# The scan's state and output products in natural order of the heads

## The chip, the cores and the metric

The kernel runs on one core of one Trainium2 chip. The metric is the device time of one run in microseconds; before the change it is 3602.42 us, the median of three runs that lie between 3598.81 and 3608.07 us. Times of instructions come from one profiled execution of the same program, counted from its first instruction.

## The reference

The reference is a small network in float32 over 512 tokens of 1024 features and a context of 256 tokens: two layers of a first block (attention with latent keys, then a gated spatial layer, each with a large MLP) and four modulated layers of a second one (convolution, recurrent layer, attention, convolution). The change lies in the recurrent layer. There each of 16 heads keeps a state S of 64 x 64, and for each token in turn, once forward over the tokens and once backward:

```
sa  = S @ (-kk_t)
S   = S * d_t  +  sa (x) (kk_t * a_t)  +  v_t (x) k_t
out = S @ r_t
```

Here d_t is a decay for each key feature, and (x) an outer product. Context tokens come first, then the others, so 768 tokens in each direction.

## The kernel before, in words

The layers run one after another. The recurrent layer writes its inputs for the scan (arrays krd, bkd, vd) to memory, and the function `wkv` reads them back and scans. It doesn't go token by token: 768 tokens are 12 chunks of 64, and within a chunk the recurrence is solved by products of matrices and the inverse of a triangular 64 x 64 matrix for each head and direction.

The work is cut into eight segments: four groups of three steps (a step is one chunk) by two halves of the heads (g, eight heads each). Both directions of a step are done side by side, each with its own chunk. Segments alternate between the halves of the heads, so that the next segment can be prepared while the present one is scanned.

`prepare` makes a segment ready. For each of its three steps it loads BK (line 1161), KR (line 1164; two loads for a direction, `for e in range(2)`, one for the place of the even heads and one for that of the odd heads in each pair) and UV (line 1155), all from the queue of SyncE. TensorE then forms G (line 1177, in two PSUM buffers) and transposes BK (line 1187); VectorE masks G into GA (line 1184). VectorE inverts the 32 x 32 diagonal blocks of all heads in a long chain of small operations (lines 1205 and 1207) between transposes of 32 x 32 (lines 1198, 1217, 1222). KR has one buffer for each half of the heads, so a load for the segment after next goes where the present segment's KR has been read for the last time.

`merge` puts the inverses of the 64 x 64 matrices together from the 32 x 32 ones with small products (lines 1233 and 1240); it needs the transposes of line 1222.

`chain` does the three steps of a segment. In each step, for both directions:

- X (lines 1264 and 1266): two products a head, accumulated in the lower 64 partitions of a PSUM tile; ScalarE copies it (line 1268).
- U (line 1271): one product a head into the upper 64 partitions, which ScalarE copies into UV (line 1272).
- S, the step of the state (line 1280): one product a head, which ScalarE scales in four pieces of two heads (line 1283) and GpSimd adds to what is left of the old state (lines 1255 and 1285).
- O, the output (lines 1288 and 1290): two products a head (one in the first step, where there is no state), copied by ScalarE (line 1292) and written out by SyncE's queue (line 1296). The last step has no S.

S and O share one tile of PSUM for each direction, `so`. Head h writes the partitions `hr(h)`: the lower 64 for an even head, the upper 64 for an odd one. In a product of TensorE the partitions of the output are the columns of its array, so even heads use columns 0 to 63 and odd heads columns 64 to 127; all 128 rows are used by both. Every product here is in float32 and shows as two records in the trace, each with a load of weights.

The order of S and O over the heads is the tuple EO (line 1121): (0, 2, 4, 6, 1, 3, 5, 7). It is used at lines 1279 and 1287.

After each step `beside` calls the generators of the next two segments' preparation, so that their work lies beside the scan. The order of instructions on each engine is set by a planner of the language when the program is built: it follows dependencies and its own costs, and may put a block of preparation into the middle of a step. In the program as built, the first G block of a preparation stands on TensorE between the first direction's X and the second direction's X of the next step, or after the first half of a merge.

Of the kernel before, what the change touches and what calls it, by code (L numbers as in the profile page):

```python
# [51 lines left out]
class Stream:  # L52
    """Pools and helpers for a chain of layers over N tokens, features on the partitions."""
# [8 lines left out]
    def pools(self, nm, wst=0, whl=0, hp=0, tp=0, mm=0, W=None, hw=None):  # L62
        """Opens the pools that are asked for by their buffers."""
# [23 lines left out]
    def wblk(self, src, cols=1024, st=None):  # L87
        """A block of weights in float32, split exactly into two float32r parts."""
        nc = self.nc
        st = self.load(src, cols) if st is None else st  # L90
        hi = self.whl.tile([P, 1024], F32R, name="wh")[:, :cols]
        lo = self.whl.tile([P, 1024], F32R, name="wl")[:, :cols]
        nc.scalar.activation(out=hi, in_=st, func=AF.Copy)  # L93
        (nc.gpsimd if self.pool_lo else nc.vector).tensor_tensor(out=lo, in0=st, in1=hi.bitcast(F32), op=ALU.subtract)  # L94
        if self.tick:
            self.tick()
        return hi, lo
# [5 lines left out]
    def split(self, pr, src, scale=None, bias=None):  # L103
        """hi + lo = src * scale, or src + bias"""
# [20 lines left out]
    def lin(self, outs, w, acts, wo=0, ws=P, start=True, stop=True):  # L125
        """outs: [(PSUM part, columns of the tokens)]"""
# [14 lines left out]
    def group(self, ws, acts):  # L141
        """Several outputs at once, as the operands become ready."""
# [6 lines left out]
    def rsqrt(self, v, pool=None):  # L149
        """v ** -0.5 on a small tile [128, n]"""  # L150
# [14 lines left out]
    def colsum(self, tiles, N):  # L165
        """Sums over the features for each token: PSUM [128 tokens, N / 128]."""
# [8 lines left out]
    def rows(self, y, N, tag="rs", dst=None):  # L175
        """Columns y [128 tokens, N / 128] -> a row over all partitions [128, N]; in PSUM without a tag."""
# [33 lines left out]
class Kern:  # L210
# [17 lines left out]
    def open_x(self, n):  # L228
        """The two streams and the running sums of their squares."""
# [12 lines left out]
    def track(self, k, vi=0, acc=None, gain=1.0):  # L242
        """x[:, k] is final: its squares go into the sum for the next norm."""
# [14 lines left out]
    def both_rstd(self, s):  # L258
        """The norms of x and of the context in one chain."""
# [18 lines left out]
    def set_filler(self, gen, per=1):  # L278
        """Another chain of work, emitted in step with the blocks of weights of the main one."""
# [14 lines left out]
    # ------------------------------------------------------------- modulation  # L294
# [7 lines left out]
    def modulation(self, s, l, pool, ps):  # L302
        """shift, scale and gate of layer l, for both vectors, with the features on the partitions"""
# [28 lines left out]
    def mod_h(self, s, x, l, vi, rs=None, gs=None):  # L332
        """The modulated norm of x, split."""
# [17 lines left out]
    # -------------------------------------------------------------- conv layer  # L351
    def conv(self, s, x, l, j, vi):
# [3 lines left out]
        with self.tc.tile_pool(name=f"cv{N}", bufs=1, side=s.side, reuse_waits="tile") as cp, \  # L356
# [5 lines left out]
            for k in range(KT):  # L362
# [10 lines left out]
                # twice a * sigmoid(b)  # L373
# [18 lines left out]
            # layer norm over the features  # L392
# [25 lines left out]
            # the norm that the next layer starts from takes the place of the sums  # L418
# [3 lines left out]
    def conv_x(self, l, j):  # L422
        """The layer on x. The convolution runs in PSUM: some taps as diagonal matrices on TensorE, most on VectorE; the last ones are for ScalarE and GpSimd."""
        nc, A, s, x, N, H = self.nc, self.A, self.m, self.x, T, 15
        NPE, NPO, NG = 4, 7, 4
        with self.tc.tile_pool(name="cv", bufs=1, reuse_waits="tile") as cp, self.tc.tile_pool(name="cw", bufs=5, reuse_waits="tile") as cw, \
# [7 lines left out]
            def glu(k):  # L434
# [7 lines left out]
                # twice a * sigmoid(b)  # L442
# [60 lines left out]
            # layer norm over the features  # L503
# [23 lines left out]
    # ---------------------------------------------------------------- block 1  # L527
    def scaled(self, gname, gi):
        """x * gain, split"""
# [15 lines left out]
    def mla(self):  # L545
        nc, tc, A, s = self.nc, self.tc, self.A, self.m
        scale = 192.0 ** -0.5
        with tc.tile_pool(name="mla", bufs=1, reuse_waits="tile") as mp, tc.tile_pool(name="mla2", bufs=2, reuse_waits="tile") as m2, \
# [10 lines left out]
            # the first products wait in PSUM for the norm  # L559
# [6 lines left out]
            # rope tables: cos and signed sin of fl(position * inv_freq)  # L566
# [160 lines left out]
    def sgu(self):  # L727
        nc, tc, A, s = self.nc, self.tc, self.A, self.m
        with tc.tile_pool(name="sgu", bufs=1, reuse_waits="tile") as sp, tc.tile_pool(name="sgu2", bufs=2, reuse_waits="tile") as s2, \
                tc.tile_pool(name="sgu8", bufs=9, reuse_waits="tile") as s8, s.pools("m", hp=8, tp=2, mm=2), tc.tile_pool(name="pa", bufs=1, space=PSUM, reuse_waits="tile") as pa:  # L730
            # spatial weights, masked, and the sums of their rows
# [76 lines left out]
    def final_norm(self, s):  # L808
        """The norm at the end of the first block, and in one step with it the norm of the layer that follows."""
# [6 lines left out]
        # r1 = (m1 + eps) ** -0.5 and r1 * (r1 ** 2 * m2 + eps) ** -0.5 = (m2 + eps * (m1 + eps)) ** -0.5  # L816
# [16 lines left out]
    # -------------------------------------------------------------- rwkv layer  # L833
    # tokens of both sequences side by side: 256 of the context, then 512 of x; two halves of 384 in two banks
# [8 lines left out]
    def headcols(self, pq, y, yw, dst):  # L843
        """y [128 tokens, 6 blocks, n heads] -> [64, 768 tokens]: rows from 0 and from 32 hold the two exact parts"""
# [10 lines left out]
    def headrows(self, pq, yr, hrow):  # L855
        """[64, 768 tokens] of headcols -> a row for each of two heads, as hrow selects them: PSUM [128, 2, 384]"""
# [5 lines left out]
    def rwkv_project(self, kd, vd, gd, bd, krd, bkd, pc, xd, xcd):  # L862
# [6 lines left out]
        with tc.tile_pool(name="pj", bufs=1, reuse_waits="tile") as pj, s.pools("r", wst=3, whl=2, mm=2), \  # L869
# [12 lines left out]
            with tc.tile_pool(name="p1", bufs=1, reuse_waits="tile") as p1:  # L882
                h = p1.tile([P, KT, TJ], F32, name="h")
                xx = p1.tile([P, KT, TJ], F32, name="xx")
                def lerp(i, half, tp):
                    """Half of the tiles: the second half takes buffers that the layer before has to leave."""
                    return [lerp1(i, k, tp) for k in range(4 * half, 4 * half + 4)]
# [25 lines left out]
                with s.pools("rn", tp=2, W=T):  # L913
                    # mu / 2 and 1 - mu for the first product, which then need not wait for xx
# [37 lines left out]
                with tc.tile_pool(name="p2", bufs=2, reuse_waits="tile") as p2:  # L952
# [18 lines left out]
                    # the values with the tokens on the partitions  # L971
# [35 lines left out]
                    # the rest of them finds its place when h and xx are gone  # L1007
                    rawp = right("raw")
                    raws = [lerp1(5, k, rawp, raw=True) for k in range(4, 8)]
            with tc.tile_pool(name="hp2", bufs=1, reuse_waits="tile") as hp2:  # L1010
# [5 lines left out]
                with tc.tile_pool(name="p3", bufs=1, reuse_waits="tile") as p3, tc.tile_pool(name="p4", bufs=2, reuse_waits="tile") as p4:  # L1016
                    def small(m):
                        """w2 and a2, split, and the rows that select the heads"""
# [6 lines left out]
                    # a running sum over each chunk starts from a zero in front of it, or behind it  # L1025
# [3 lines left out]
                    # a0 / 2, w0 / 2, k_a / 2 and 1 - k_a / 2, and the constant of the decay  # L1029
# [28 lines left out]
                    def chunks(m, k, r, wa):  # L1058
                        pr = self.headrows(pq, kyr, wa[0][:64, 256:])
                        # half of the normalised k  # L1060
# [41 lines left out]
                        # bonus: sum over the head of r * (both k) * r_k, times v, left for the scan that has the time  # L1102
# [13 lines left out]
    def wkv(self, vd, bd, krd, bkd, pc, od, osp):  # L1116
        nc, tc = self.nc, self.tc
        NS, NU = 3, 24
        # where the inverses pause
        CUT = (10, 20)  # L1120
        EO = (0, 2, 4, 6, 1, 3, 5, 7)
        chunk = lambda d, st: st if d == 0 else (3 - st if st < 4 else 15 - st)
        states, kept, first, last = {}, {}, [], {}
        with ExitStack() as c:
            pool = lambda n, b, **k: c.enter_context(tc.tile_pool(name=n, bufs=b, **k, reuse_waits="tile"))
            # the order of the pools puts what the first segment starts with where the layer before leaves first
# [7 lines left out]
            def prepare(g, b):  # L1134
                # 24 units forward, 8 that stay empty, 24 backward
                if b == 0:
# [3 lines left out]
                    # the two heads of a tile on the diagonal  # L1140
# [10 lines left out]
                def values(i):  # L1151
                    # V below an empty U
# [5 lines left out]
                for i in range(NS):  # L1158
# [6 lines left out]
                    # those of the first segment are behind all else that it loads  # L1165
# [5 lines left out]
                    for d in range(2):  # L1171
                        mask = self.c("mrev" if d else "mfwd")
                        for mm in range(2):
# [8 lines left out]
                            # nothing slows the inverses that the first step waits for  # L1182
# [8 lines left out]
                # inverses of the 32 x 32 diagonal blocks, one for a partition  # L1191
# [20 lines left out]
                for d in range(2):  # L1212
# [6 lines left out]
                    # the other orientation of the block that the merge starts from  # L1219
# [24 lines left out]
            def chain(beside, g, b, GA, KR, BT, UV, TP):  # L1244
                hr = lambda h: slice(64 * (h % 2), 64 * (h % 2) + 64)
                for i in range(NS):
                    st = NS * b + i
                    S0 = [states.get((g, d)) for d in range(2)]
                    # what is left of the state after this step
# [8 lines left out]
                    for d in range(2):  # L1258
                        # X in the lower half of the partitions, U in the upper
                        X = pch.tile([P, 8, 64], F32, name=f"xu{d}")  # L1260
                        xu.append(X)
                        for h in range(8):
                            # the rows of U are still zero
# [9 lines left out]
                    for d in range(2):  # L1273
                        cc = chunk(d, st)
                        u0 = d * 32 + 8 * i
                        # the step of the state, and the output
# [31 lines left out]
            # the bonus in place, beside the first inverses  # L1308
# [20 lines left out]
            for n, sg in enumerate(segs):  # L1329
                # the last step of the next segment and the start of its inverses  # L1330
# [16 lines left out]
    def rwkv_readout(self, gd, bd, od, last, xd, xcd):  # L1347
# [3 lines left out]
        # the order of the pools puts what the first half of the heads needs where the last segment of the scan has nothing,  # L1351
        # so that it runs beside the scan
        with ExitStack() as c:
# [23 lines left out]
            # the sums of squares of each head, for both halves of the heads  # L1377
            pk = s.mmt()[:, :96].rearrange("p (g b h) -> p g b h", g=2, h=8)

            def centre(g, m, pq):  # L1380
# [6 lines left out]
                # the centred o takes its place  # L1387
# [12 lines left out]
            def readout(g, i):  # L1400
                m = 4 * g + i
                # the backward o is no longer needed
# [499 lines left out]
```

## Time and profile before

| | |
|---|---|
| median of 3 runs | 3602.42 us |
| profiled execution, first to last instruction | 3582.6 us |
| TensorE busy in the profiled execution | 3409.4 us (95%) |
| VectorE busy | 2307.9 us (64%) |
| ScalarE busy | 1448.9 us (40%) |
| the scan's steps, about | 2135 to 2565 us of the span |

The profile gives no other time for the profiled execution than its span; the runs' times include what lies before the first and after the last instruction. A busy time is the union of an engine's instructions. Ends of TensorE's products are modelled, and they overlap, so a busy TensorE need not be one that works at its full rate: the distance between starts tells the rate. The clock is the share of TensorE's full clock that was granted. In a timeline, instructions of one form that follow each other are one row with their count, and a row ends with the engine's idle time before it and with what ended it.

### The profile page before, as it was taken

The numbers are of one execution on the slowest core, as the hardware profiler recorded it, in microseconds if no ns is written. First come the engines' busy times: TensorE is split into PE (matmuls) and PEld (weight loads), VectorE is DVE, ScalarE is ACT, GpSimd is POOL, SyncE is SP. The second block draws the span as 40 slices with busy tenths as digits, with TensorE's granted clock in tenths as the row PEclk, the third lists the DMA queues.
The fourth block names the chain that finished last, engine by engine and source line by source line (L and its number), as shares of the span: only waits on it lengthen the run. The fifth ranks groups of instructions, "written<-read, shape, count | busy, mean of one in ns | idle before, by whom it ended". The sixth has DMA issues, their size and how long they took to land. (4 is left out here: it accounts for less than half of the span.)

```text
span 3582.6 us, 52130 instructions
## 1 busy us (share of the span) xinstructions
PE 3409.4 (95%) x20784; PEld 2778.1 (78%) x20784; DVE 2307.9 (64%) x3811; ACT 1448.9 (40%) x2336; POOL 603.8 (17%) x674
## 2 busy tenths in 40 slices
PE   7999999999999999998999979999889999999897
PEld 4678888767766787676988858888788788888676
DVE  4568875426443345887478788888452476666786
ACT  3443334323232233555356524333423254444553
POOL 1000000000000000763002231121110200000682
PEclk9999999999999999998999879999899999999999
DMA  6123333343444322221227772221421522211221
GB/s 246 44 89 107 111 117 113 136 142 136 152 143 157 120 98 94 71 77 65 95 101 227 240 208 82 84 87 49 175 92 42 182 71 80 71 62 46 91 73 57
DMA packets 201380, 396.94 MB, mean 111 GB/s; under 512 B 16624, under 2 KB 109552, under 8 KB 200112
## 3 DMA queue, kind: packets, MB, share of 16 engines
q1 hardware_dynamic: 161328, 287.56, 24.0%
q0 software_dynamic: 24880, 93.08, 7.8%
q10 hardware_dynamic: 14928, 12.98, 1.2%
q8 instruction: 163, 2.67, 0.3%
q14 instruction: 81, 0.66, 0.1%
HBM read 328.79 MB, written 58.46 MB: 108 GB/s over the span
## 5 line engine op out<-in xcount | busy, mean ns | idle before, releaser
L93 ACT ACTIVATE wh<-wst 128x1024 fp32r<-128x1024 f32 (+1 forms) x413 | 423.0, 1026 | 1100.5 <-PE pmm L122 728.8
L121 PE MATMUL pmm<-hh,wh 128*128 128x512 f32 (+1 forms) x1752 | 670.5, 384 | 4.2 <-ACT hh L108 3.6
L123 PE MATMUL pmm<-hh,wl 128*128 128x512 f32 (+1 forms) x1752 | 662.3, 379 | 4.3 <-POOL wl L94 4.3
L122 PE MATMUL pmm<-hl,wh 128*128 128x512 f32 (+1 forms) x1752 | 661.5, 378 | 2.7 <-DVE hl L109 1.9
L94 DVE TENSOR_TENSOR wl<-wst,wh 128x1024 fp32r<-128x1024 f32 (+1 forms) x347 | 406.8, 1173 | 348.8 <-ACT wh L93 348.3
L121 PEld LDWEIGHTS pmm<-hh,wh 128*128 128x128 f32 x1752 | 332.0, 190 | 90.5 <-ACT wh L93 13.4
L123 PEld LDWEIGHTS pmm<-hh,wl 128*128 128x128 f32 x1752 | 331.1, 189 | 73.1 <-POOL wl L94 6.0
L122 PEld LDWEIGHTS pmm<-hl,wh 128*128 128x128 f32 x1752 | 331.3, 189 | 67.5 <-issue 5.3
L465 DVE SCALAR_TENSOR_TENSOR acc<-yp,vec,acc 128x512 f32<-128x512 f32 x320 | 224.5, 751 | 20.6 <-PE acc L461 14.1
L94 POOL TENSOR_TENSOR wl<-wst,wh 128x1024 fp32r<-128x1024 f32 x66 | 161.5, 2460 | 425.7 <-ACT wh L93 405.3
L539 DVE TENSOR_TENSOR x<-pmm,x 128x512 f32<-128x512 f32 x88 | 60.7, 690 | 247.7 <-PE pmm L123 247.7
L121 PE MATMUL pmm<-uh,wh 128*128 128x512 f32 x512 | 200.5, 392 | 0.0
L123 PE MATMUL pmm<-uh,wl 128*128 128x512 f32 x512 | 199.7, 390 | 0.0
L122 PE MATMUL pmm<-ul,wh 128*128 128x512 f32 x512 | 199.3, 389 | 0.0
L84 POOL DMA_DIRECT2D wst<-mod_w x96 | 50.8, 530 | 562.7 <-PE pmod L312 512.4
L312 PE MATMUL pmod<-wst,cs 128*32 128x512 f32 x384 | 110.5, 657 | 19.1 <-DMA wst<-mod_w 18.9
L474 POOL TENSOR_TENSOR part<-part,tap 128x512 f32<-128x512 f32 x96 | 124.0, 1292 | 13.8 <-ACT part L472 7.5
L708 DVE SCALAR_TENSOR_TENSOR ft<-pmm,rs 128x512 f32<-128x512 f32 x64 | 44.0, 688 | 118.4 <-PE pmm L123 117.0
L381 DVE SCALAR_TENSOR_TENSOR Y<-yp,vec,Y 128x256 f32<-128x256 f32 x240 | 115.7, 482 | 6.2
L121 PEld LDWEIGHTS pmm<-uh,wh 128*128 128x128 f32 x512 | 96.2, 188 | 26.4 <-ACT wh L93 7.5
L123 PEld LDWEIGHTS pmm<-uh,wl 128*128 128x128 f32 x512 | 96.1, 188 | 20.2
L1177 PE MATMUL G<-KR,BK 128*128 128x256 f32 x384 | 102.0, 410 | 10.1 <-DMA KR<-krd 6.6
(673 smaller groups left out, 7503.5 us busy)
## 6 DMA issues: line engine op xcount, KB each, us to landing
wst<-mod_w POOLq DMA_DIRECT2D x96, 512.0 KB, 4.0
wst<-w_up SPq DMA_DIRECT2D x64, 512.0 KB, 3.2
wst<-w_down SPq DMA_DIRECT2D x64, 512.0 KB, 3.2
wst<-conv_in SPq DMA_DIRECT2D x48, 512.0 KB, 3.2
wst<-conv_in POOLq DMA_DIRECT2D x24, 512.0 KB, 3.6
BK<-bkd SPq DMA_DIRECT2D x48, 256.0 KB, 2.9
KR<-krd SPq DMA_DIRECT2D x96, 128.0 KB, 3.3
krd<-kr SPq DMA_DIRECT2D x14, 768.0 KB, 4.3
```

Of the source, the lines that this page charges most:

```text
L84: self.dma.dma_start(out=st, in_=src)
L93: nc.scalar.activation(out=hi, in_=st, func=AF.Copy)
L94: (nc.gpsimd if self.pool_lo else nc.vector).tensor_tensor(out=lo, in0=st, in1=hi.bitcast(F32), op=ALU.subtract)
L121: nc.tensor.matmul(out, w[0], a[0], start=start, stop=False)
L122: nc.tensor.matmul(out, w[0], a[1], start=False, stop=False)
L123: nc.tensor.matmul(out, w[1], a[0], start=False, stop=stop)
L312: nc.tensor.matmul(pm[n // 4][32 * q:32 * q + 32, :], self.cs[:, k, :], w[:, h * 512:(h + 1) * 512], start=k == 0, stop=k == KT - 1, skip_ ...
L381: nc.vector.scalar_tensor_tensor(out=acc, in0=yp[:, i:i + N], scalar=wc, in1=acc, op0=ALU.mult, op1=ALU.add)
L465: nc.vector.scalar_tensor_tensor(out=accs[k], in0=yps[k][:, i:i + N], scalar=weight(k, i), in1=accs[k], op0=ALU.mult, op1=ALU.add)
L474: nc.gpsimd.tensor_tensor(out=part, in0=part, in1=t, op=ALU.add)
L539: self.nc.vector.tensor_tensor(out=self.x[:, m], in0=pt, in1=self.x[:, m], op=ALU.add)
L1177: nc.tensor.matmul(G[:, 2 * q:2 * q + 2].rearrange("p e x -> p (e x)"), BK[:, d, i, m].rearrange("p a t -> p (a t)"), KR[:, d, i, m].rearr ...
```

## The change

Line 1121 gives EO another value, so that S and O take the heads in the order 0 to 7. Even and odd heads then follow each other, and with them the two halves of the columns. Everything else in the change removes comments and doc strings, with line numbers kept.

```diff
@@ wkv
         # where the inverses pause
         CUT = (10, 20)
-        EO = (0, 2, 4, 6, 1, 3, 5, 7)
+        EO = range(8)
         chunk = lambda d, st: st if d == 0 else (3 - st if st < 4 else 15 - st)
```

## Rows read from the trace of the kernel before

**Rows 1.** The first line of the page: span and instructions.
```profile
span 3582.6 us, 52130 instructions
```
**Rows 2.** Stretches of the scan: length, busy PE, PEld, DVE, ACT, POOL; granted clock, DMA share, GB/s.
```profile
2135.00:2565.00 430.00, 411.71 (x6261) 371.90 (x6259) 338.39 (x574) 165.31 (x422) 77.51 (x109) 0.95 0.25 81
2186.00:2468.00 282.00, 271.13 (x4132) 243.14 (x4132) 247.17 (x417) 107.13 (x280) 53.90 (x73) 0.98 0.26 80
```
**Rows 3.** Waits from 2135 to 2565: us in total, times, longest.
```profile
DVE GA L1184 <- PE G L1177: 30.2, 23, 2.9
...
PE so L1288 <- ACT S L1283: 8.1, 19, 0.5
```
**Rows 4.** Timeline of TensorE's products: S of one step and X after it.
```profile
2315.66 1.37 PE L1280 MATMUL so<-UV,BT 128*64 128x64 f32 x29
2316.81 0.27 PE L1264 MATMUL xu<-UV,GA 128*64 128x64 f32 x1
2316.86 0.22 PE L1280 MATMUL so<-UV,BT 128*64 128x64 f32 x1
2316.92 0.22 PE L1264 MATMUL xu<-UV,GA 128*64 128x64 f32 x1
2316.92 0.22 PE L1280 MATMUL so<-UV,BT 128*64 128x64 f32 x1
```
**Rows 5.** Timeline of TensorE's products: O of the same step and X after it.
```profile
2317.64 0.33 PE L1288 MATMUL so<-GA,UV 128*64 128x64 f32 x2 [0.39 <-ACT S L1283]
...
2318.27 0.28 PE L1290 MATMUL so<-KR,S 128*64 128x64 f32 x2
2318.39 0.34 PE L1288 MATMUL so<-GA,UV 128*64 128x64 f32 x4
2318.51 0.33 PE L1290 MATMUL so<-KR,S 128*64 128x64 f32 x4
...
2319.14 0.34 PE L1288 MATMUL so<-GA,UV 128*64 128x64 f32 x4
...
2320.66 0.27 PE L1266 MATMUL xu<-S,KR 128*64 128x64 f32 x1
```
**Rows 6.** Timeline of ScalarE: the scalings of the same step's S.
```profile
2316.66 1.74 ACT L1283 ACTIVATE S<-so,pc 128x64 f32<-128x64 f32 x8 [0.78 <-PE so L1280]
```
**Rows 7.** Timeline of SyncE's queue: the loads of KR after this step.
```profile
2318.82 1.35 SPq L1164 DMA_DIRECT2D KR<-krd  x2
...
2321.96 1.26 SPq L1164 DMA_DIRECT2D KR<-krd  x2
```
**Rows 8.** DMA issues from 2150 to 2500: count, KB each, median us to landing.
```profile
KR<-krd SPq DMA_DIRECT2D x64, 128.0 KB, 2.9
```
**Rows 9.** Timeline of TensorE's products: first G block after three steps.
```profile
2171.76 1.53 PE L1177 MATMUL G<-KR,BK 128*128 128x256 f32 x6 [1.37 <-DMA KR<-krd]
...
2322.90 1.99 PE L1177 MATMUL G<-KR,BK 128*128 128x256 f32 x8
...
2357.43 1.75 PE L1177 MATMUL G<-KR,BK 128*128 128x256 f32 x7 [0.81 <-DMA KR<-krd]
```
**Rows 10.** Timeline of TensorE's products: two merges, and the G in one.
```profile
2296.43 1.70 PE L1233 MATMUL tr<-TP,GA 32*32 32x32 f32 x48
2297.94 1.45 PE L1240 MATMUL tr<-GA,TP 32*32 32x32 f32 x40
2299.32 1.99 PE L1177 MATMUL G<-KR,BK 128*128 128x256 f32 x8
...
2515.39 0.78 PE L1233 MATMUL tr<-TP,GA 32*32 32x32 f32 x19 [4.24 <-DVE TP L1222]
```
**Rows 11.** Timeline of VectorE: transpose of the first direction ahead of a merge.
```profile
2290.59 1.99 DVE L1222 STREAM_TRANSPOSE TP<-LW 32x1024 f32<-32x1024 f32 x1
```
**Rows 12.** Stretches, with the columns of Rows 2: around a wait, and a drop.
```profile
2170.00:2180.00 10.00, 8.63 (x84) 7.17 (x82) 6.73 (x17) 1.77 (x3) 0.00 (x0) 1.00 0.36 114
2307.90:2311.30 3.40, 3.40 (x35) 3.40 (x34) 3.35 (x3) 0.59 (x1) 0.00 (x0) 0.50 0.00 0
```

## The prediction

> **What bounds the kernel now.** I read the page's first part for the whole (a span of 3582.6 us [rows 1]), then the stretches of the scan [rows 2], then who waits for whom there [rows 3], and last, instruction by instruction, one step of the scan on TensorE, ScalarE and the loading queue, and the ends of segments [rows 4 to 11]. The reader is to see that TensorE is the engine that paces the scan (411.7 of 430 us busy in it) and that VectorE is not far behind (247.2 of 282 us in the five segments from 2186 to 2468). So time taken off TensorE counts, but little can be taken off before something else is late.
>
> A step of the scan (12 steps, two halves of the heads, so 24 in all) runs on TensorE as X, U, S (line 1280), O (lines 1288, 1290). A product is two records. Inside one half of the columns records start every 0.058 us: an x2 row of O is followed by the next after 0.116 [rows 5]. When the other half's first products come within reach, the halves run at once: the x4 rows hold twice the records in the same 0.116, and at the end of S records of X (lower half) and of S (upper half) alternate, each half still at 0.058 [rows 4]. But this holds for the last four records of a half only: even heads of O start at 2317.64, odd ones at 2318.39, the next direction's even ones at 2319.14, and X after both directions at 2320.66, so 16 records cost 0.75 us, not 16 x 0.058 = 0.93. In S four blocks of 8 records take 2315.66 to 2316.81, 0.29 each.
>
> **The change part by part.** No instruction and no transfer is added or removed; the products of S and of O only change places. With heads in natural order a product of the other half is always next or next but one, within the reach of four records seen above, so I take both halves to run at 0.058 throughout.
>
> *S.* The first direction's last record now starts 0.74 us after the first (0.29 + 0.05 for a first load + 7 x 0.058); then 0.05 + 7 x 0.058 = 0.46. ScalarE's four scalings wait for all eight heads: they start at 2316.66 after idling for S, though heads 0 and 1, which the first of them reads, were through by 2316.3 (odd heads start at 2315.66 + 0.29, two records and 0.22 to the end of a record) [rows 4, 6]. O in turn waits for the scalings (19 waits on TensorE [rows 3]) and starts 0.98 us after ScalarE began. So O begins 0.28 us earlier. TensorE's own end of S moves by more (0.35), which only lengthens the idle 0.39 before O. The second direction's scalings (1.74 us for eight) end 0.2 before its O is reached.
>
> *O.* From 2317.64 to X at 2320.66 are 3.02 us; then 32 records in each half, 32 x 0.058 + 0.05 = 1.91. Saving 1.11.
>
> *What is late next.* O is the last reader of KR, and its end releases the load of KR for the segment after next. That load feeds G (line 1177), which stands in TensorE's queue behind the first direction's X, and X's second direction, U and S are queued behind G. The two loads of a direction (even heads' place, odd heads' place) are issued at 2318.82 and, as the pair takes 1.35 with 0.6 each, at about 2319.57 [rows 7]. The even heads end no earlier than before: their 16 records take 0.05 + 15 x 0.058 from O's start either way. So the first load is issued at the same distance from O's start, and the second follows at the queue's own pace (the other direction's pair takes 1.26, so 0.66 apart instead of 0.75): 0.07 to 0.09 earlier. With 2.9 us to landing [rows 8] it lands near 4.75 us after O's start, and I let G start 0.1 after that (a guess at how long a wait takes to end), at 4.85. TensorE reaches G 5.26 us after O's start now (2322.90, no wait [rows 9]) and would at 4.15. So a step that doesn't wait today keeps 0.4 of the 1.11, and a step that waits already keeps 0.07. Ten steps have such a G; four of these start late by 0.35 to 1.4 (one, of 1.37, stands in [rows 9]); so 6 x 0.4 + 4 x 0.07 = 2.7 us. Bounds for one step: 0.07 and 1.11; I stay by the measured landing.
>
> Six steps end a segment: between O and G there stand 2.9 us of the merge (2296.43 to 2299.32 [rows 10]), and the load has landed. There O's 1.11 is kept, if VectorE's transposes for the merge are there. Where those for the first direction end at 2292.6, 3.8 before the merge, they are [rows 11]. I count three steps in full; the other three at 0.25 each (one already waits 0.81 for KR [rows 9]; two more I take like it, because VectorE, idle for 34.8 of 282 us [rows 2], will not follow everywhere): 3 x 1.11 + 0.75 = 4.1 us.
>
> The segment from 2468 to 2515 ends with TensorE waiting 4.24 us for VectorE [rows 10]: what its three steps save (2 x 1.39 + 1.11 = 3.9) only lengthens this wait. Zero.
>
> The last segment has no G and no inverses on VectorE: 3 x 1.11 = 3.3. The first steps of the first two segments have no state yet, so O has half the records: 0.2 each, 0.4.
>
> S's 0.28 falls in 22 steps, less the two in the segment that waits for VectorE: 20 x 0.28 = 5.6.
>
> Sum: 5.6 + 0.4 + 2.7 + 4.1 + 3.3 = 16.1 us. The profiled span of 3582.6 becomes 3566.5. The runs' median 3602.4 lies 19.8 above that span, outside of what changes: 3586.
>
> *Not shown in the trace:* the two halves alternating for longer than four records. Below I bound it from no overlap at all (a loss) to 0.029 per record over both halves; 32-column products on one tile already come every 0.031 (48 records in 1.51 us up to the next group [rows 10]), so TensorE can take records nearly that fast. I take full overlap, since rows 4 show both halves at full pace.
>
> The Trainium skill speaks against this ("TensorE: Matmul & The Clock Gate", Part 3, The mechanism and what overlaps): a weight load overlaps a product in flight only if the row group differs, and here both halves use all 128 rows. The trace disagrees as far as it goes: S and X at 2316.8 to 2317.0 load and multiply side by side in the same rows [rows 4]. By that rule the sum would be the loss of rival C.
>
> **Rivals.**
> A, *KR's load is not in the way*: G is moved by the planner, or loads land earlier with a queue that is less crowded, and the ten steps keep 1.11 as well, the six merge steps too: 16 x 1.11 + 3.3 + 5.6 + 0.4 = 27.1 us, 3575. For it: VectorE is idle for 34.8 us in the five segments [rows 2], and over the scan it waits 30.2 for G [rows 3], so it can start earlier. Against: G already waits for KR in some steps.
> B, *O gains nothing before the last segment*: the loads or VectorE take all of it; 5.6 + 3.3 = 8.9, 3593.5. For it: VectorE's 88% in the five segments (247.2 / 282); a mask that comes late holds the second G.
> C, *the halves take turns*: products of the other half don't run under one in flight unless they were already waiting. Then O is 64 x 0.058 + 0.05 = 3.76 (0.74 more) and S's first direction ends after 0.92 instead of 0.74. 19 full steps and 2 half ones outside the waiting segment: 19 x 0.74 + 2 x 0.3 + 20 x 0.18 = 18 us slower, 3621. It decides once a record costs more than about 0.047 over both halves, today's mean in O (3.02 / 64). Against: rows 4 and 5.
> D, *the clock*: TensorE waits 0.6 us more at each of ten G's and its granted clock drops in each. A drop as at 2307.9 lasts 3.4 us at a granted 0.50 (1.2 GHz) with TensorE busy throughout [rows 12], half of which is lost: ten times 1.7, the gain is gone, 3603. For it: the clock already stands at 0.95 over the scan, with such drops in it [rows 2]. Against: the wait of 1.37 for KR at 2171.76 brought none, the stretch around it stands at 1.00 [rows 12].
>
> **How the numbers follow.** Forecast 0.50; A 0.15; B 0.17; C 0.10; D 0.08. A measurement of this kernel can tell about 0.3% (10.8 us) from no change. Faster by over that: most of the forecast case (0.43), A, a part of B: 0.60. Within: the rest of these and D: 0.27. Slower: C, and some weight for a planner that orders the rest less well: 0.13. The range 3570 to 3606 holds the forecast, A, B and D and leaves out C and a gain beyond A's. The likeliest case alone is 3581 to 3592.
>
> **What would show it.** S in 0.98 us and O in 1.91 us from first record to the next X, with x4 or single alternating rows throughout; O's wait for ScalarE starting 0.28 us earlier; KR's pair issued 1.2 us after O's start as now; G waiting for KR in nearly all ten steps, some 0.6 us each; the wait for the transposes at 2515 grown by 3 to 4 us. O longer than 3.02 us means C; no waits at G means A. The prediction is wrong if the planner changes the order of TensorE's queue elsewhere, which no row of before can show.

## The result, and the profile after

The change makes the kernel faster: a median of 3582.2 us over 11 runs (3570.81 to 3590.26) beside 3607.02 over 11 runs of the kernel before on the same chip (3588.28 to 3620.07). The ratio of the two on record is 0.9948, with a 95% interval of 0.9930 to 0.9965: 18.8 us less, between 12.6 and 25.2. The two medians alone lie 24.8 apart, at the far end of that interval. A second set of 12 runs (e5 below) gave 0.9943 [0.9924, 0.9962]. The forecast was 3586.

The page of the changed kernel begins with the span and with each engine's busy time, share and instructions. The count of instructions is that of [rows 1].

```profile
span 3575.3 us, 52130 instructions
...
PE 3388.1 (95%) x20784; PEld 2755.5 (77%) x20784; DVE 2307.4 (65%) x3811; ACT 1446.7 (40%) x2336; POOL 603.2 (17%) x674
```

PE is busy for 21.3 us less than before and its weight loads (PEld) for 22.6 less; VectorE, ScalarE and GpSimd are busy for what they were, within 2.2. The spans differ by only 7.3 us, less than the medians do: in every case with a listed profiled run the profile's span lies 1.7 to 1.8 below that run's time, so the execution behind the profile of before took some 3584.4, under each of the 92 runs of that kernel that stand beside the results (3587.24 to 3627.24). A second profile of it (e10) has a span of 3612.9.

The same stretches as in [rows 2], and the one after them; columns as there.

```profile
2135.00:2565.00 430.00, 399.76 (x6460) 354.68 (x6458) 348.05 (x587) 172.34 (x435) 80.39 (x113) 0.94 0.29 93
...
2186.00:2468.00 282.00, 263.19 (x4253) 232.46 (x4249) 250.73 (x420) 107.77 (x286) 54.02 (x74) 0.95 0.27 83
2468.00:2515.00 47.00, 39.84 (x760) 37.78 (x759) 43.94 (x75) 17.34 (x43) 7.82 (x12) 0.86 0.31 103
```

In the same 282 us PE is busy for 8 us less while 121 more records start, and VectorE for 3.6 more: more of the scan fits in, and VectorE is busy for 89% of the stretch instead of 88%. Now one step on TensorE, the one after the merge at 2297 [rows 4, 5]:

```profile
2316.12 1.15 PE L1280 MATMUL so<-UV,BT 128*64 128x64 f32 x32
2317.10 0.40 PE L1264 MATMUL xu<-UV,GA 128*64 128x64 f32 x4
2317.83 0.34 PE L1288 MATMUL so<-GA,UV 128*64 128x64 f32 x4 [0.33 <-ACT S L1283]
2318.00 0.29 PE L1290 MATMUL so<-KR,S 128*64 128x64 f32 x4
2318.12 0.33 PE L1288 MATMUL so<-GA,UV 128*64 128x64 f32 x4
...
2319.63 0.34 PE L1290 MATMUL so<-KR,S 128*64 128x64 f32 x4
2319.75 0.28 PE L1266 MATMUL xu<-S,KR 128*64 128x64 f32 x2
2319.87 0.28 PE L1264 MATMUL xu<-UV,GA 128*64 128x64 f32 x2
```

All of O is now x4 rows at 0.116 us, 0.029 for a record. From O's start to the next X are 1.92 us (3.02 before), from S's start to X 0.98, from S's start to O 1.71 (1.98). The next direction's X, which uses one half only, is back at x2 rows, 0.058 for a record. On ScalarE the scalings start 0.73 after S does, not 1.00 [rows 6]; on SyncE's queue the loads of KR start 1.18 after O does, as before [rows 7]:

```profile
2316.85 1.74 ACT L1283 ACTIVATE S<-so,pc 128x64 f32<-128x64 f32 x8 [0.51 <-PE so L1280]
```

```profile
2319.01 1.30 SPq L1164 DMA_DIRECT2D KR<-krd  x2
...
2321.52 1.27 SPq L1164 DMA_DIRECT2D KR<-krd  x2
```

The first G blocks of four steps, where [rows 9] had one without a wait (a block has 8 records; x1 and x2 are what short windows held of it). The row of 2322.72 names a VectorE instruction as the releaser, but the trace has the second load of KR land at 2322.62, 0.10 before:

```profile
2173.88 0.67 PE L1177 MATMUL G<-KR,BK 128*128 128x256 f32 x2 [1.14 <-DMA KR<-krd]
...
2270.50 0.45 PE L1177 MATMUL G<-KR,BK 128*128 128x256 f32 x1 [1.14 <-DMA KR<-krd]
...
2285.90 0.45 PE L1177 MATMUL G<-KR,BK 128*128 128x256 f32 x1 [0.63 <-DMA KR<-krd]
...
2322.72 1.97 PE L1177 MATMUL G<-KR,BK 128*128 128x256 f32 x8 [0.59 <-DVE LW L1207]
```

Waits from 2135 to 2565 (total, times, longest), to be read against [rows 3], and the wait at the merge that was 4.24 long in [rows 10]:

```profile
DVE GA L1184 <- PE G L1177: 23.1, 23, 6.6
...
PE tr L1233 <- DVE TP L1222: 8.7, 3, 6.9
PE so L1288 <- ACT S L1283: 7.9, 17, 0.6
...
PE G L1177 <- DMA KR<-krd: 5.3, 6, 1.1
```

```profile
2508.83 2.60 PE L1233 MATMUL tr<-TP,GA 32*32 32x32 f32 x45 [6.87 <-DVE TP L1222]
```

VectorE waits less for G (23.1 for 30.2), TensorE more for VectorE and for KR. (The row for KR holds five of the ten first G's; the other five stand under VectorE, like that of 2322.72, though each starts 0.10 to 0.14 after its load has landed. All ten sum to 8.9 us, 2.7 before.) The order of instructions on ScalarE, GpSimd and SyncE is that of before; on TensorE and VectorE the planner moved some. In the ten steps with a G after X, 38 records of X start between O and the first G block, 36 before, so one product of X more stands ahead of it; some merges are split elsewhere. (X has 64 records for both directions, so in either kernel this G stands inside the second direction's X, and not ahead of it as the description of the kernel has it.)

### The profile page after: what moved, and what is told of

It reads as the page before. It is cut to its first block, busy times and chain, and to the rows that moved or that the text cites. A ratio compares the mean times of both kernels' runs of the same rounds, so it can differ in the third digit from the quotient of the medians.

```text
span 3575.3 us, 52130 instructions
## 1 busy us (share of the span) xinstructions
PE 3388.1 (95%) x20784; PEld 2755.5 (77%) x20784; DVE 2307.4 (65%) x3811; ACT 1446.7 (40%) x2336; POOL 603.2 (17%) x674
## 5 line engine op out<-in xcount | busy, mean ns | idle before, releaser
L465 DVE SCALAR_TENSOR_TENSOR acc<-yp,vec,acc 128x512 f32<-128x512 f32 x320 | 224.5, 752 | 20.5 <-PE acc L461 14.1
```

The lines of the kernel that those rows point to most:

```text
L465: nc.vector.scalar_tensor_tensor(out=accs[k], in0=yps[k][:, i:i + N], scalar=weight(k, i), in1=accs[k], op0=ALU.mult, op1=ALU.add)
```

## Experiments

Each ratio is to runs of the kernel before on the same chip. "Full-clock time" is a run's time multiplied by its mean granted clock, so that a us at half clock counts as half a us; waits at full clock count in full. For one kernel it scatters far less than the time (standard deviation over the 12 runs of e5: 4.2 us against 9.0), so what differs from run to run is mostly the clock. It is 3463.0 (33 runs), 3462.9 (31) and 3464.3 (17) for the kernel before on three chips, and 3440.0 for the change.

**e1, S alone in natural order.**

```diff
-                        for h in EO:    # S, line 1279
+                        for h in range(8):
```

> Natural order in S alone, O still even heads first. My theory (TensorE's two halves overlap; O starts when ScalarE has scaled S): S takes 0.93 us from first to last start instead of 1.32, O starts 1.71 us after S instead of 1.98, nothing else moves, about 20 steps keep 0.28 us: 5.6 us less than before (0.16%), so too small to be told by time alone. Rival (what helps is the planner's other order of TensorE's queue, not the halves): the queue's order here is that of before, so no step gets shorter.

Median 3597.22 (12 runs), ratio 0.9983 [0.9968, 0.9997]: 6 us less (1 to 12), and 4.9 by full-clock time. In its profile S takes 0.93 us from first to last start in 17 of 22 steps (1.32 before), O stays at 3.19. The order of instructions is that of before on every other engine, and G stands where it stood in X, so this is the alternation and nothing else.

**e2, O alone.**

```diff
-                        for h in EO:    # O, line 1287
+                        for h in range(8):
```

> Natural order in O alone, S still even heads first. My theory: O takes 1.85 us to the next X instead of 3.02, but in the ten steps with a G block after X that block waits for the load of KR (starting 4.8 to 5.7 us after O's start) and keeps 0.3 of the 1.1; in all 10.5 us less than before (0.3%). Rival (all of O's 1.1 us counts in every step): 21 x 1.1 = 23 us less, and no waits at G.

Median 3588.32 (10 runs), ratio 0.9956 [0.9942, 0.9970]: 16 us less (11 to 21), more than the 10.5 expected and less than the rival's 23. O's first and last starts are 1.91 apart (3.19 before), S's 1.32 as before. VectorE's order and G's place in X are those of the whole change, so e2 holds the planner's moves too; they are not separated from O.

**e3, pairs of heads.**

```diff
-        EO = (0, 2, 4, 6, 1, 3, 5, 7)
+        EO = (0, 2, 1, 3, 4, 6, 5, 7)
```

> Both S and O in the order 0 2 1 3 4 6 5 7, so a half of the columns keeps TensorE for 4 records in S and 8 in O. My theory (a half starts when its record is among the next four): S as in the change, 0.93 us; O one block of 8 records per 0.05 + 4 x 0.058 = 0.28 us, eight blocks, 2.3 us to the next X; the ten G blocks wait for KR as with the change, so the time is near that of the change, some 14 us less than before. Rival (the halves are kept busy whatever the order, as soon as they alternate): O 1.85 us. Rival (a switch of halves costs something by itself): O below 1.85.

Median 3596.12 (10 runs), ratio 0.9969 [0.9953, 0.9986]: 11 us less, and 15.2 by full-clock time, where 14 were expected. The timeline of its O:

```profile
2328.33 0.33 PE L1288 MATMUL so<-GA,UV 128*64 128x64 f32 x2 [0.37 <-ACT S L1283]
2328.50 0.28 PE L1290 MATMUL so<-KR,S 128*64 128x64 f32 x2
2328.61 0.34 PE L1288 MATMUL so<-GA,UV 128*64 128x64 f32 x4
2328.73 0.33 PE L1290 MATMUL so<-KR,S 128*64 128x64 f32 x4
2328.90 0.34 PE L1288 MATMUL so<-GA,UV 128*64 128x64 f32 x4
2329.02 0.34 PE L1290 MATMUL so<-KR,S 128*64 128x64 f32 x4
2329.19 0.34 PE L1288 MATMUL so<-GA,UV 128*64 128x64 f32 x4
```

From O's start to the next X are 2.30 us (2.3 expected). Eight records of a half cost 0.29, about half way between the 0.23 of the natural order and the 0.38 of the old blocks of sixteen (0.75). That is what a reach of about four waiting records gives, read off [rows 4, 5], for all three lengths of a block (4, 8 and 16 records of a half).

**e4, KR's second load on ScalarE's queue** (on top of the change), so that it need not follow the first.

```diff
-                            nc.sync.dma_start(out=KR[r, d, i, :, e], in_=krd[d][cc, r, gs])
+                            (nc.scalar if b and e else nc.sync).dma_start(out=KR[r, d, i, :, e], in_=krd[d][cc, r, gs])
```

> The change, with the second of KR's two loads of a direction (odd heads' place, from the second pair of segments on) issued by ScalarE's queue instead of SyncE's, so that it need not stand 0.7 us behind the first. My theory (KR's load is what the first G waits for): G starts 0.4 to 0.7 us earlier after O's start in the ten steps, 4.2 to 4.6 instead of 4.75 to 5.8, and the time falls by 4 to 6 us below that of the change (some 20 to 24 less than before). Rival (VectorE's masks, or the second direction's load, decide): G's first block moves but the steps keep their length, the time is that of the change.

A miss: 3606.21 (12 runs), ratio 1.0006 [0.9990, 1.0022], the whole gain gone. By full-clock time it is 3444.4, only 4 us above the change; the mean clock is 0.9550 for 0.9603, and that is where most of the gain went. Its DMA issues (count, KB, median us to landing) and its waits from 2135 to 2565:

```profile
KR<-krd SPq DMA_DIRECT2D x32, 128.0 KB, 3.4
KR<-krd ACTq DMA_DIRECT2D x32, 128.0 KB, 3.9
```

```profile
PE G L1177 <- DMA KR<-krd: 11.7, 12, 2.1
```

The second load goes out 1.33 after O's start instead of 1.87, but the two then travel together and take longer (3.0 median in the change). In the ten steps it lands 5.02 after O's start in the mean, 5.06 in the change, and TensorE waits 8.5 us at their first G blocks, 8.9 in the change. In the six merge steps it waits 6.2 us for KR, 0.7 in the change. The planner also moved more of VectorE's instructions than for the change. The merge steps grew from 143.3 to 158.0 us, 51 of them at half clock (31 in the change); the profile is that of the slowest of the 12 runs. So e4 shows that this route brings the load no earlier; why its clock is lower, and what an earlier load would give, it does not show.

**e5, the change once more**, with the next three on one chip.

```diff
-        EO = (0, 2, 4, 6, 1, 3, 5, 7)
+        EO = range(8)
```

> The change itself (comments kept), beside the next three on the same chip. 0.5 to 0.6% less than before, some 20 us. My theory of the spread: a run's time times its mean granted clock is nearly one number for a kernel (before: 3463, the change: 3440), so that what differs from run to run is the clock; it should come out at 3440 again. Rival: the product spreads as much as the time does.

Median 3582.92 (12 runs), ratio 0.9943 [0.9924, 0.9962]; full-clock time 3441.3, where 3440 was expected.

**e6, the change with G behind both directions' X.** The preparation pauses after its loads; what follows them is called after both X's and no longer at the step's end.

```diff
+                    yield LOADED            # in prepare, after a step's loads
...
+                    after_x(i)              # in chain, between X and U
...
                 def beside():
                     if beside.i < NS - 1:
                         next(prs[n + 2], None)
-                        for _ in range(1):
-                            next(prs[n + 1], None)
                     beside.i += 1
+                def after_x(i):
+                    if i:
+                        next(prs[n + 2], None)
+                        adv(prs[n + 1])
```

> The change, with G of the next but one segment put behind both directions' X instead of between them (loads issued where they were). My theory (with the change TensorE stands some 0.6 to 0.9 us at G in ten steps, for KR's load): X's second direction, 1.9 us, covers the load, no waits for KR at G's first block, each of ten steps shorter by 0.5 to 0.9, 4 to 9 us below the change, if the clock stays. Rival (VectorE is the bound by now, and a later G delays its masks): steps no shorter, the wait goes to the merges.

Median 3577.78 (8 runs), ratio 0.9916 [0.9888, 0.9944], the best version of all: 30 us less than before (20 to 40). By medians it lies 5.1 below e5 on the same chip, and the two intervals overlap; by full-clock time it lies 12 below (3429.2), with a mean clock of 0.9586 for 0.9601. The timeline of one step whose O starts at 2315.63 (line 1275 is X, 1186 is G, 1281 is U):

```profile
2319.18 0.40 PE L1275 MATMUL xu<-S,KR 128*64 128x64 f32 x4
...
2321.14 1.99 PE L1186 MATMUL G<-KR,BK 128*128 128x256 f32 x8
2323.07 1.49 PE L1281 MATMUL xu<-Xs,GA 64*64 64x64 f32 x22
2325.14 1.99 PE L1186 MATMUL G<-KR,BK 128*128 128x256 f32 x8 [0.58 <-DVE GA L1193]
```

G comes 5.51 after O's start without a wait. So it is, within 0.1, in six of the ten steps with a G; in the other four it still waits for KR, 2.6 us in all. The ten steps sum to 146.9 us, 157.7 in the change.

**e7, X and U on both halves too** (on top of the change): the first direction's X in the lower half and the second's in the upper, U the other way round, the directions alternating head by head.

```diff
+                    px, pu = (slice(0, 64), slice(64, 128)), (slice(64, 128), slice(0, 64))
-                    for d in range(2):
-                        for h in range(8):
...
+                    for h in range(8):
+                        for d in range(2):
...
-                            nc.tensor.matmul(X[0:64, h], GA[:, d * 32 + 8 * i + h, 0], ...
+                            nc.tensor.matmul(xu[d][px[d], h], GA[:, d * 32 + 8 * i + h, 0], ...
```

> The change, and X and U on both halves too: X of the backward direction goes to the upper 64 partitions and its U to the lower, the directions alternating product by product. My theory: X of both directions takes 1.9 us instead of 3.8, U 1.0 instead of 1.9; in the ten steps with G that waits for KR and for VectorE's masks most of it is given back; the last segment keeps 2.6 us a step, so 8 us there and up to 12 in the others, 5 to 20 below the change in full-clock work; the waits may lower the clock and take some back. Rival (what limits is only TensorE's products): 24 steps x 2.6 = 60 us below the change.

Median 3589.82 (12 runs), ratio 0.9954 [0.9935, 0.9974]: no more than the change alone, with a median 6.9 above that of e5. Against before, the full-clock time fell by 52 us (3462.9 to 3410.8), but the mean clock from 0.9607 to 0.9501. The stretches of [rows 2] in its profile:

```profile
2186.00:2468.00 282.00, 249.00 (x4230) 211.61 (x4227) 251.58 (x419) 107.49 (x286) 54.76 (x74) 0.88 0.28 83
2468.00:2515.00 47.00, 36.30 (x694) 32.12 (x693) 42.69 (x75) 15.75 (x40) 8.41 (x13) 0.79 0.23 81
```

The ten steps with G fell to 133.9 us, the six merge steps rose to 171.0, 74 of them at half clock. One merge of them, on TensorE, and three stretches around it:

```profile
2304.58 1.67 PE L1233 MATMUL tr<-TP,GA 32*32 32x32 f32 x48 [2.86 <-DVE TP L1222]
```

```profile
2302.00:2304.00 2.00, 0.00 (x0) 0.00 (x0) 1.97 (x2) 0.22 (x1) 1.31 (x2) 1.00 0.58 175
...
2306.00:2308.00 2.00, 2.00 (x42) 1.84 (x40) 1.99 (x2) 0.97 (x3) 0.00 (x0) 0.75 0.56 159
2308.00:2310.00 2.00, 2.00 (x7) 1.55 (x6) 2.00 (x2) 0.00 (x0) 0.00 (x0) 0.50 0.04 8
```

TensorE, early at the merge, waits 2.86 us for VectorE's transposes; after 2306 its clock falls, to 0.50 (1.2 GHz), while it is busy throughout. Such waits sum to 25.4 us in this kernel's scan, the time at half clock from 2140 to 2560 to 113 us (8.7 and 55 in the change). That the waits bring the drops is argued from the order in which they stand, here and at the change's longest wait below; it is not shown. In e4 the time at half clock rose to 85 us with only 3.3 us of such waits, and the drop of [rows 12] at 2307.9 follows 11 us in which TensorE was busy throughout.

**e8, e7 with G later.** The edits of e6 and e7 together.

> X and U on both halves, and G behind X. My theory: VectorE becomes the bound in the segments with inverses (some 50 us each of 53 now), so little below the kernel with X and U on both halves alone, 0 to 5 us. Rival (KR's load at G is what takes X's and U's gain away): 10 to 20 us below it.

Median 3590.03 (12 runs), ratio 0.9962 [0.9939, 0.9985]; full-clock time 3409.3, clock 0.9497. What G later gave in e6 gives nothing here: the ten steps even take 138.8 us, 133.9 in e7.

**e9, the kernel before with G later.** e6's edit with the old EO.

> The kernel before (even heads first) with G of the next but one segment behind both directions' X, as in the run with G later. My theory (the load of KR is late at G only because O is short): before, O's 3.0 us and one direction's X cover the load in most steps, so G later can win back only the waits that are there, four of 0.35 to 1.4 us, 2 to 3 us in all (less than 0.1%), against some 10 us with the change. Rival (a later G is simply the better place): 10 us less than before here too.

Median 3594.26 (12 runs), ratio 0.9966 [0.9946, 0.9985]: 12 us less (5 to 19), and 12.6 by full-clock time. My theory that G later pays only where a short O makes the load late fell here: the ten steps go from 165.9 to 156.1 us, as much as from the change to e6. The timeline of a step of e9 whose O starts at 2323.95, lines as in e6:

```profile
2330.40 0.28 PE L1275 MATMUL xu<-S,KR 128*64 128x64 f32 x2
2330.61 1.99 PE L1186 MATMUL G<-KR,BK 128*128 128x256 f32 x8
2332.54 0.91 PE L1281 MATMUL xu<-Xs,GA 64*64 64x64 f32 x12
```

G begins 6.66 after O's start, without a wait, and U stands between its blocks. Of the 9.8 us at most 3.5 were waits for KR in the kernel before; so G between the two X's costs some 0.6 us in a step apart from KR. How much of that are the changes between records of X and G, and how much the second G's wait for VectorE's masks of the first (line 1184), no run separates.

**e10, the kernel before, profiled again.** No edit.

> The kernel before, unchanged, for a second profile. The question is whether TensorE's granted clock in the scan differs between before and the change: the first profile of before has 31 us at 0.50 between 2140 and 2560, the two of the change 55 and 61. If it is the change that lowers the clock (waits at G), this profile has about 31 again; if it is chance, it may have 50 or more.

One run, 3614.71 us. The scan from 2140 to 2560, columns as in [rows 2]:

```profile
2140.00:2560.00 420.00, 400.93 (x6020) 361.70 (x6017) 337.12 (x570) 156.04 (x403) 75.45 (x104) 0.93 0.26 81
```

Of these 420 us TensorE spent 58.0 at half clock; in the first profile of the same program 41.6, at a mean of 0.95. (The 31 of the expectation leaves out a drop that began at 2133.8 and lasted to 2150.9.) The change's two profiles have 54.6 and 61.4, both 0.93: one profile of the kernel before has more than one of the change, so no difference is shown that would need a cause in the change.

## Why the prediction was right

By parts, from O's first start in one step to that in the next, in us. Two profiles of each kernel, since one alone differs by 7 in the sum. The column "at full clock" takes off half of the time that a part stood at half clock (in the merge steps 13.7 and 27.3 us before, 30.7 and 27.3 in the change); like full-clock time it is an estimate.

| part | before, e10 | change, e5 | difference of means | at full clock | predicted |
|---|---|---|---|---|---|
| first steps of two segments | 28.8, 28.7 | 26.9, 27.3 | -1.6 | -1.8 | -1.0 |
| ten steps with G after X | 165.9, 166.7 | 157.7, 159.4 | -7.7 | -7.7 | -5.5 |
| six steps with a merge | 143.1, 149.1 | 143.3, 141.4 | -3.8 | -8.0 | -5.8 |
| segment around 2468 to 2515 | 48.7, 48.9 | 47.5, 49.4 | -0.4 | -2.1 | 0 |
| last segment, with its last O | 23.9, 23.9 | 21.4, 21.4 | -3.7 | -3.7 | -3.9 |
| sum | | | -17.2 | -23.3 | -16.1 |

(The predicted column puts S's 0.28 to each of its 20 steps; the last row adds 1.2 for O of the last step, an estimate between the 1.11 to the next X and the 1.28 by which O's last start moves.) The sum at full clock is what the runs show for the whole kernel: 3463.0 to 3440.0, 23 us.

*S* was right: O begins 0.27 earlier (0.28 predicted), and S alone is worth 6 us (5.6). *O's size* was right: wherever X follows at once it starts 1.91 or 1.92 us after O (1.91), in one step 2.0. Rival C is out: the halves run side by side for the whole of O, at 0.029 a record, where it needed 0.047.

The rule of the Trainium skill that spoke for C ("TensorE: Matmul & The Clock Gate", Part 3, The mechanism) is therefore not what these rows show for column halves: all rows of O load weights and multiply in the same 128 rows at once. The same section of the Trainium skill says that products start strictly in program order; here X's first record starts at 2316.81, ahead of records of S at 2316.86 and 2316.92 [rows 4]. 29 records of S start before it, so it starts between the two records of one product of S.

*KR's load* was right in its mechanism and nearly in its price. The loads go out at 1.18 and 1.87, the second lands between 4.6 and 5.64, and G starts 0.10 to 0.14 after the landing in all ten steps (4.75 to 5.74): rival A, where nothing waits, is out for these steps. G's start is 5.19 in the mean (5.30 in e5), 5.56 and 5.57 before; the forecast comes to 5.29, with 4.85 where G had not waited and some 5.9 where it had. So O's part is 3.2 us (2.7 forecast) and S's 2.7 (2.8). The other 1.8 of the 7.7 lie between G and the next S, where I had put nothing. The product of X that now stands ahead of G, in time in which TensorE would wait, makes some 1.2 of it (ten times two records of 0.058, an estimate). Rival B is out by the same sum.

*The merge steps* were undersized, and the time hides it: 3.8 of 5.8, within what two profiles of one kernel differ by there (143.1 and 149.1). At full clock the profiles agree (136.3 and 135.5 before, 127.9 and 127.7 in the change), and each of the six steps is 1.2 to 1.5 shorter: nearly all of the 1.39 that S and O save. So the three steps for which I kept 0.25 of O's 1.11 kept about all of it; for the merge steps rival A was right.

*The segment that waits for VectorE* was right at zero in time. Its first two steps fell from 10.71 and 8.66 to 9.29 and 7.63, and the wait grew from 4.24 to 6.87 (4.4 in e10, 8.7 in e5). The stretches around that wait in the change:

```profile
2500.00:2504.00 4.00, 1.96 (x64) 1.82 (x62) 3.66 (x13) 1.30 (x3) 0.60 (x1) 1.00 0.33 87
2504.00:2508.00 4.00, 0.00 (x0) 0.00 (x0) 3.94 (x3) 0.00 (x0) 0.95 (x2) 0.65 0.89 311
2508.00:2512.00 4.00, 3.17 (x63) 3.17 (x64) 3.94 (x3) 0.85 (x2) 0.53 (x1) 0.50 0.92 368
```

The clock falls inside the wait and comes back only after 2524. Beside the longer wait stands a longer drop: 20.5 us at half clock in both profiles of the change, 17.1 in both of before. That costs 1.7 of the 2.1 us that the segment saves at full clock: rival D, in the one place where I had not put it, and small. At the ten G's, where I had, none of the two profiles of the change has any time at half clock. Two of the steps, with waits of 0.59 and 0.94 at G:

```profile
2317.83:2348.96 31.13, 28.59 (x428) 24.78 (x428) 29.35 (x59) 11.49 (x33) 7.34 (x10) 1.00 0.33 103
```

The mean clock over runs agrees: 0.9603 and 0.9601 with the change, 0.9605 to 0.9607 without.

*The first steps* saved 0.8 each in place of 0.5, since their O, with half the records, gained more than the 0.2 I gave it: its starts span 2.0 us (2.4 once in e5), 2.6 and 2.7 before.

*What was wrong beside a size:* that the median "lies 19.8 above that span, outside of what changes". Only 1.8 lies outside; the rest is the clock of a lucky execution. By the medians of 3605 to 3608 that 33, 31 and 17 runs gave, 16.1 less is 3589 to 3592: I was 3 to 5 low on the base and, with medians of 3582 and 3583, 6 to 9 short on the gain (3 to 4 by the ratios). The two errors go against each other, so that the forecast came within 4 us is in part luck. The whole change (18.8 and 20.6 us) is about S alone plus O alone (6 + 16), so the shortfall lies in O's term (10.5 forecast without S). By the column at full clock 2.2 of it lie in the ten steps, 2.2 in the merge steps, 2.1 in the segment that waits for VectorE and 0.8 in the first steps.

*Left open:* what the planner's own moves on TensorE gave (e2 holds them with O), why the ten steps with a short O gain 0.8 to 0.9 each and not the 1.39 that S and O save even with G later (e9 to e6: 156.1 to 146.9, where the four waits that e6 still has explain 2.6 of the missing 4.7), and whether the drops of the clock come from the waits. A second place for KR, which would let its load start before O ends, was not tried.

## What to carry to other kernels

Products that fill one half of TensorE's columns run two at a time if the other half's next product stands within about four records in the queue: alternate the halves record by record, and test it by the x4 rows of the timeline. Before the saving is summed up, look for what TensorE reaches earlier: a load that is released by the shortened work itself goes out no earlier, and a wait for a second engine that is nearly as busy can take most of a segment's saving (0.4 of 3.9 us came through in the segment around 2468 to 2515). Compare variants by time and by time times granted clock: where the second falls and the first does not, as in e4 and e7, work is gone and a lower clock has taken its place. In e7 and e8 more overlap on TensorE bought nothing beyond the change; whether a faster VectorE would alter that, no run shows.

## What the runs showed of the hardware that was not expected

- Time multiplied by mean granted clock is nearly a constant of a kernel (3462.9 to 3464.3 on three chips, with medians of 3605 to 3608), so e1's gain of 4.9 us can be read from it (standard deviation of its 12 runs 3.0), where the times of the same runs have a standard deviation of 7.3.
- Two loads of 128 KB sent out together landed after 3.4 and 3.9 us in the median, against 3.0 when sent 0.7 apart on one queue (e4): a second queue brought the later one hardly any earlier, 5.02 us after O's start for 5.06.
- Taking TensorE's full-clock time down by 52 us (e7) gave no more time than 23 us did, with the clock a hundredth lower.
